# Seven products instead of eight in thirteen more places of a two-layer decoder trunk

## The chip, the cores and the metric

The kernel runs on one core of a Trainium2 chip. The metric is device time in microseconds of that core for one launch. Engines are named as the profile names them: PE is TensorE (matmul), PEld its weight loads, DVE is VectorE, ACT is ScalarE, POOL is GpSimd, SP is SyncE, whose queue issues the DMAs. PSUM is the accumulator memory that PE writes, in eight banks of 128 x 512 fp32.

## The reference

Two layers of a decoder on x of 256 rows by D = 2048, all in fp32. The first mixes with a gated short convolution, the second with stick-breaking attention of 16 heads; each is followed by a squared-ReLU MLP with a hidden width of 4 D. Keys and values are made once, after the first layer.

```
def short_conv_mixer(u, w_in, conv_w, w_out):            # layer 0
    xin, gate_c, gate_b = jnp.split(u @ w_in, 3, axis=-1)
    ...
    return (gate_b * conv) @ w_out
def sq_relu_mlp(u, w_up, w_down):
    return jnp.square(jax.nn.relu(u @ w_up)) @ w_down
def reference(...):
    for i in range(2):
        u = rmsnorm(h, mix_pre_g[i])
        m = short_conv_mixer(u, ...) if i == 0 else stick_breaking_mixer(u, w_q, k_sh, v_sh, w_o)
        h = h + rmsnorm(m, mix_post_g[i])
        u = rmsnorm(h, mlp_pre_g[i])
        h = h + rmsnorm(sq_relu_mlp(u, w_up[i], w_down[i]), mlp_post_g[i])
        if i == 0:
            k_sh, v_sh = split(rmsnorm(h, kv_norm_g) @ w_kv)
```

## The kernel before, in words

**Products.** fp32 numbers are split into a high part that PE takes exactly and a low part. A *product* is three 128 x 512 matmuls into one PSUM bank: high by high, high by low, low by high. Of each 128 x 1024 weight tile that arrives by DMA (`raw`, names `r...`), ACT makes the high part (`h...`, a rounding copy) and DVE the low part (`l...`, the subtraction). `hu`, `lu` belong to the up weights, `hd`, `ld` to the down weights, `hin`, `hout`, `hv`, `hk`, `hq`, `hwo` to the others. High and low parts have six pages each (`SLOTS`), so DVE and ACT can be at most six pages ahead of PE.

**Groups.** A `Group` computes 256 rows by 1024 columns over 2048 rows of a weight: two row blocks b, two column halves c, sixteen weight tiles, so 64 products into four banks `acc`. The groups run one after the other: six `in` groups, two `out`, then for each layer's MLP four quarters of two up groups and two down groups (`u<layer><quarter><group>`, `d...`), between the layers the value groups `v0` and `v1`, eight narrower groups for k and q, and two `wo` groups. In the kernel before, `v0` comes ahead of the k and q groups and `v1` behind them.

**Seven products.** Two weight tiles by two row blocks make a 2 x 2 block product, for which `seven` uses seven products instead of eight, with sums of operands: of the data (forms `us`, `hs`, `ys`, made once per norm or hidden tile by `make_forms`) and of the weights (`t1` to `t4`, made by DVE for every pair of tiles). A "seven" in this text is such a pair; an "eight" is an ordinary tile with four products, so two eights stand for one seven. Four of the seven products go to four extra banks `q`, so a group with sevens fills all eight banks. After a group's last seven `combine` makes the sums of the q banks on ACT and DVE, and after its last product `finals` adds them to `acc` on the way out. The lists `UP_SEVEN`, `DN_SEVEN` and so on say which of the eight pairs of a group are sevens; `turns` spreads them among the eights, with `FORE` eights ahead and `REAR` behind.

**First and last groups.** The first group behind a norm (`enter`) starts with its first four tiles (`EDGE`) for row block 0 alone, since row block 1 is not ready yet. The last group ahead of a norm (`leave`) does its last four tiles bank by bank, so that the norm can begin on the first banks while PE works on the others. In the kernel before, neither kind has sevens, nor do `v0`, `v1` and `wo`.

**Order.** `Plan` is a list scheduler that runs when the kernel is built: every instruction is a task with an estimated duration and a due time, and the plan fixes the order on each engine. On the chip each engine goes through its list in that order.

Lines of the profile: L643 is the matmul of a product, L407 every ACT instruction, L415 every two-operand DVE instruction, L422 DVE's form with a scalar, L466 the transposes.

Of the kernel before, what the change touches and what calls it, by code (L numbers as in the profile page):

```python
# [88 lines left out]
class Plan:  # L89
# [13 lines left out]
    def task(self, eng, dur, fn, reads=(), writes=(), side=False, soon=None, kb=0.0, table=None, own=(), after=()):  # L103
# [3 lines left out]
        t.preds, t.succs, t.allocs, t.kb, t.table, t.side = set(after), [], [], kb, table, side  # L107
# [59 lines left out]
    def place(self):  # L167
# [52 lines left out]
        while done < len(tasks):  # L220
# [39 lines left out]
            if e in ("SP", "POOL") and t.kb:  # L260
# [3 lines left out]
                t.end = dma + 1.9  # L264
# [59 lines left out]

UP_SEVEN = ((0,1,2,4),(0,1,2))
IN_SEVEN = (0,1,2)
OUT_SEVEN = (0,1,2)
DN_SEVEN = ((0,1,2,4),)*2
SUMS_BY_DMA = ()
# [4 lines left out]
UP_DMA = ((),)*2  # L334
IN_DMA = ()
OUT_DMA = ()
LO_DMA = "lo"
DN_DMA = ((),)*2
# [3 lines left out]
def trunk(ctx, tc, x, xT, vecs, rows, ws, hs, qs, out):  # L342
# [165 lines left out]

    def raw_page(name):
        return page("raw", [P, CW], F32, name)  # L510

    def split(raw, name, a=0, b=CW, parts=1, gains=None):
        hi, lo = page("hi", [P, CW], F32R, "h" + name), page("lo", [P, CW], F32R, "l" + name)
# [92 lines left out]
    def make_forms(XS, pairs, r0, r1, name, spare):  # L606
# [14 lines left out]
        for j in pairs:  # L621
# [11 lines left out]
            if place is None:  # L633
                XS["late"].append(last)
            else:
                last()
# [12 lines left out]
    class Group:  # L649


        def __init__(self, name, w, base, n, X, banks, evict, ks=1, gains=None, XS=None, sevens=(), seeds=None, qbanks=None, start=None, bydma=(), qin=None, qout=None):
            self.qin, self.qout = qin, qout
            self.bydma = bydma
            self.name, self.w, self.base, self.n, self.X, self.banks, self.evict = name, w, base, n, X, banks, evict
            self.ks, self.gains, self.XS, self.sevens, self.seeds, self.qbanks = ks, gains, XS, sevens, seeds, qbanks
            self.start, self.fine, self.on, self.before_out = start, 0, None, None
# [41 lines left out]
        def seven(self, j, last):  # L699
# [3 lines left out]
            if j in SUMS_BY_DMA:  # L703
                rs = page("rs", [P, CW], F32, f"r{name}s")
                r1 = page("r2", [P, HALF], F32, f"r{name}b")
                twice = w[base + 1][:, HALF:].unsqueeze(1).to_broadcast([P, 2, HALF])
                load(rs.col().as3("p (a n) -> p a n", a=2), twice)
                load_add(rs.col(), w[base])
                load(r0.col(), w[base])
                load(r1.col(), w[base + 1][:, :HALF])  # L710
                b22, b21, t1, t2, t4 = r0.col(HALF, CW), r1.col(), rs.col(0, HALF), r2.col(0, HALF), r2.col(HALF, CW)
                at = {"t1": (rs, 0), "t3": (rs, 1), "t2": (r2, 0), "t4": (r2, 1), "b21": (r1, 0)}
            else:
                r1 = raw_page(f"r{name}b")
                r3 = page("r2", [P, HALF], F32, f"r{name}d")
                load(r0.col(), w[base])
                load(r1.col(), w[base + 1])
                b11, b22, b21, b12 = r0.col(0, HALF), r0.col(HALF, CW), r1.col(0, HALF), r1.col(HALF, CW)
                t1, t2, t4 = r2.col(0, HALF), r2.col(HALF, CW), r3.col()
# [880 lines left out]
```

## Time and profile before

| | |
|---|---|
| time, median of three runs | 2111.51 us (2111.33 to 2111.85) |
| time of the profiled execution | 2110.88 us |
| span in its trace | 2109.2 us |
| granted clock of PE | 0.999 |
| PE busy | 2093.5 us, 99% |
| PEld busy | 1737.5 us, 82% |
| DVE busy | 1867.1 us, 89% |
| ACT busy | 1346.0 us, 64% |
| DMA | 429.67 MB, mean 204 GB/s |

Busy time is the union of an engine's instructions. The span runs from the first to the last instruction of the trace; the time of the execution has 1.7 us around it. Matmuls overlap each other in the records, so a mean duration (some 390 ns) is not the distance from one to the next, which the chain of waits gives.

### The profile page before, as it was taken

Reading aid. Unit: us, or ns where it says so; the run is one execution under the profiler, and the core shown is the slowest. Engines: PE = TensorE matmul, PEld = TensorE weight load, DVE = VectorE, ACT = ScalarE, POOL = GpSimd, SP = SyncE. Lnnn points to the kernel's source line nnn. Section 1 sums busy time; section 2 is a strip of 40 time slices with the busy share of each in tenths; the row PEclk is TensorE's granted clock in tenths of the full one; section 3 lists DMA queues with packets and bytes.
Section 4 is the critical chain, followed back from the end, with each engine's and each line's share of the span. In section 5 each row is a group of like instructions: output and inputs, shape, how many; then the busy total and the mean of one; then the engine's idle time right before and its main releaser. Section 6 shows DMA issues by size and latency. Waiting matters only on the chain.

```text
span 2109.2 us, 27197 instructions
## 1 busy us (share of the span) xinstructions
PE 2093.5 (99%) x9506; PEld 1737.5 (82%) x9506; DVE 1867.1 (89%) x2646; ACT 1346.0 (64%) x1933; POOL 1.0 (0%) x7
## 2 busy tenths in 40 slices
PE   8999999999999999999999999999999999999998
PEld 7888888888888888888888888888888888888886
DVE  6999996899999999999657777558999999999995
ACT  7665566765666575577657776447655765665673
POOL 0000000000000000000000000000000000000000
PEclk9999999999999999999999999999999999999999
DMA  8556676556656656657664555755566566656673
GB/s 330 196 194 201 209 257 221 178 185 216 200 184 212 204 190 204 216 189 279 226 193 158 163 164 174 236 189 200 185 198 228 181 198 203 218 180 201 200 269 120
DMA packets 119801, 429.67 MB, mean 204 GB/s; under 512 B 13296, under 2 KB 13424, under 8 KB 119664
## 3 DMA queue, kind: packets, MB, share of 16 engines
q1 hardware_dynamic: 119520, 427.87, 60.9%
q8 instruction: 74, 1.21, 0.2%
q14 instruction: 63, 0.52, 0.1%
q10 hardware_dynamic: 144, 0.07, 0.0%
HBM read 419.50 MB, written 8.39 MB: 203 GB/s over the span
## 4 chain that ended last, share of the span: by engine, by line
PE 98%; DVE 1%; ACT 0%; issue 0%; DMA 0%; DVEq 0%; ACTq 0%
PE acc L643 79%; PE q L643 16%; PE tr L466 2%; PE o L1424 0%; PE z L1374 0%; DVE lv L422 0%; DVE hh L422 0%; PE ex L1404 0%; ACT hid L407 0%; PE o L1425 0%; PE z L1375 0%; DMA gv<-vecs 0%; DVE u L415 0%; PE ex L1405 0%; ACT hu L407 0%
## 5 line engine op out<-in xcount | busy, mean ns | idle before, releaser
L643 PE MATMUL acc<-hu,u 128*128 128x512 f32 x1472 | 471.4, 392 | 0.0
L643 PE MATMUL acc<-hd,hid 128*128 128x512 f32 x1376 | 437.7, 391 | 0.0
L643 PEld LDWEIGHTS acc<-hu,u 128*128 128x128 f32 x1472 | 276.4, 188 | 56.4
L643 PEld LDWEIGHTS acc<-hd,hid 128*128 128x128 f32 x1376 | 258.5, 188 | 52.8
L643 PE MATMUL acc<-lu,u 128*128 128x512 f32 x736 | 286.7, 390 | 0.0
L643 PE MATMUL acc<-ld,hid 128*128 128x512 f32 x688 | 268.0, 389 | 0.0
L415 DVE TENSOR_TENSOR lu<-ru,hu 128x1024 fp32r<-128x1024 f32 x160 | 193.2, 1221 | 17.1 <-ACT hu L407 16.6
L407 ACT ACTIVATE hu<-ru 128x1024 fp32r<-128x1024 f32 x160 | 167.4, 1058 | 45.8 <-PE acc L643 31.2
L643 PE MATMUL acc<-hin,u 128*128 128x512 f32 x588 | 186.6, 393 | 5.8 <-ACT hin L407 5.8
L415 DVE TENSOR_TENSOR ld<-rd,hd 128x1024 fp32r<-128x1024 f32 x144 | 173.6, 1219 | 19.8 <-ACT hd L407 19.5
L407 ACT ACTIVATE hd<-rd 128x1024 fp32r<-128x1024 f32 x144 | 149.1, 1052 | 40.5 <-PE acc L643 34.4
L643 PEld LDWEIGHTS acc<-lu,u 128*128 128x128 f32 x736 | 138.4, 188 | 27.5
L643 PEld LDWEIGHTS acc<-ld,hid 128*128 128x128 f32 x688 | 129.3, 188 | 26.2
L643 PEld LDWEIGHTS acc<-hin,u 128*128 128x128 f32 x588 | 111.2, 189 | 28.8 <-ACT hin L407 6.1
L643 PE MATMUL acc<-lin,u 128*128 128x512 f32 x294 | 115.3, 392 | 0.0
L415 DVE TENSOR_TENSOR q<-acc,q 128x512 f32<-128x512 f32 x130 | 87.1, 689 | 7.4 <-PE acc L643 5.6
L415 DVE TENSOR_TENSOR q<-q,q 128x512 f32<-128x512 f32 x136 | 92.7, 682 | 0.5 <-ACT q L407 0.3
L643 PE MATMUL q<-hd,hs 128*128 128x512 f32 x240 | 92.1, 389 | 0.0
L643 PE MATMUL acc<-hk,u 128*128 128x512 f32 x256 | 86.6, 399 | 0.0
L415 DVE TENSOR_TENSOR lin<-rin,hin 128x1024 fp32r<-128x1024 f32 (+1 forms) x72 | 80.1, 1129 | 4.5 <-ACT hin L407 4.2
L643 PE MATMUL acc<-hv,u 128*128 128x512 f32 x256 | 82.9, 394 | 0.1
L407 ACT ACTIVATE hin<-rin 128x1024 fp32r<-128x1024 f32 (+1 forms) x72 | 69.8, 984 | 19.8 <-PE acc L643 9.9
(1656 smaller groups left out, 4476.1 us busy)
## 6 DMA issues: line engine op xcount, KB each, us to landing
ru<-w_up SPq DMA_DIRECT2D x160, 512.0 KB, 4.3
rd<-w_dn SPq DMA_DIRECT2D x144, 512.0 KB, 4.5
rin<-w_in SPq DMA_DIRECT2D x64, 512.0 KB, 4.7
rv<-w_v SPq DMA_DIRECT2D x32, 512.0 KB, 4.2
rk<-w_k SPq DMA_DIRECT2D x32, 512.0 KB, 4.2
rq<-w_q SPq DMA_DIRECT2D x32, 512.0 KB, 3.9
rwo<-w_wo SPq DMA_DIRECT2D x32, 512.0 KB, 4.3
rout<-w_out SPq DMA_DIRECT2D x26, 512.0 KB, 4.6
```

What stands on the lines that cost most here:

```text
L407: nc.scalar.activation(out_.w(), in_.r(), func, scale=val(scale), **more)
L415: "DVE", dve(width(out_)), lambda: nc.vector.tensor_tensor(out_.w(), a.r(), b.r(), op=op),
L466: nc.tensor.matmul(to.w(), src.r(), ident.tile[:], is_transpose=True, start=j == 0, stop=True, skip_group_check=True)
L643: nc.tensor.matmul(ps.w(), a.w(), w.w(), start=first and j == 0, stop=last and j == 2, skip_group_check=skip)
```

## The change

**Where sevens are added.** `UP_FIRST`: pair 7 of the first up group of each layer. `FIRST_SEVEN` is empty, so the first `in` group stays without. `OUT_LEAVE` and `DN_LEAVE`: pairs 0 and 1 of the last `out` group and of the last down group of each layer. `V_SEVEN`: pairs 3 to 7 of `v1`. That is 2 + 2 + 4 + 5 = 13. The up groups keep their number of sevens but on other pairs. (`UP_SEVEN[0]` goes from 0, 1, 2, 4 to 3, 5, 6, 7, `UP_SEVEN[1]` from 0, 1, 2 to 5, 6, 7.)

**Leaving groups with sevens.** In a group that leaves, `fold` has DVE add the combined sums to `acc` in PSUM, in place, ahead of the last four tiles; PE then accumulates on top.

**Weight sums.** One DVE instruction over 1024 columns, one of its inputs read twice, makes `t1` and `t3`; `t2` replaces the input. The product of q7 moves from fifth to second place and that of q6 from second to fifth, and the last two stay.

**Values and attention.** `v1` runs directly behind `v0`. Its norm `kv` gets forms for pairs 3 to 7 (high plus low part of the operand, then `make_forms`), and each seven of `v1` first has ACT scale the two raw tiles by the norm's gains in four pieces. All heads' outputs (`mixed`) are made within the k and q groups, where the last eight stood at the end of `v1`; the attention's buffers `lb` shrink from eight to six.

**What moves in the lists.** VectorE's list at the first seven of the second `in` group (`rin10a`, `rin10b` are the two raw tiles, `rin10c` the page of the wide sums, `rin10d` that of the last sum), before:

```order
L415 TENSOR_TENSOR rin10c<-rin10b,rin10a 128x512
L415 TENSOR_TENSOR rin10c<-rin10c,rin10a 128x512
L415 TENSOR_TENSOR rin10b<-rin10b,rin10a 128x512
L415 TENSOR_TENSOR rin10d<-rin10c,rin10b 128x512
L415 TENSOR_TENSOR lin_664<-rin10c,hin_652 128x1024
```

and now:

```order
L427 TENSOR_TENSOR rin10c<-rin10b,rin10a 128x1024
L427 TENSOR_TENSOR rin10b<-rin10c,rin10a 128x512
L427 TENSOR_TENSOR rin10d<-rin10b 128x512
L427 TENSOR_TENSOR lin_663<-rin10c,hin_646 128x1024
L427 TENSOR_TENSOR lin_681<-rin10a,hin_670 128x1024
```

Two narrow sums have become one wide one; every seven of the kernel has this change, old ones too.

VectorE's list behind the last tiles of `v0`, before, where the k group (`lk`) follows:

```order
L422 SCALAR_TENSOR_TENSOR lv_9764<-rv_9652,gv,hv_9754 128x1024
L422 SCALAR_TENSOR_TENSOR lv_9782<-rv_9660,gv,hv_9772 128x1024
L422 SCALAR_TENSOR_TENSOR lk_9798<-rk_9675,gv,hk_9790 128x512 x2
L422 SCALAR_TENSOR_TENSOR lk_9818<-rk_9702,gv,hk_9812 128x512 x2
L422 SCALAR_TENSOR_TENSOR lk_9838<-rk_9720,gv,hk_9832 128x512 x2
```

and now, in `v1`, the sevens of pairs 5 and 6, the second and third of four that follow each other without an eight between them (`rv15a` is the first raw tile of pair 5 in `v1`):

```order
L427 TENSOR_TENSOR lv_10073<-rv14d,hv_10067 128x512
L427 TENSOR_TENSOR rv15d<-rv15b 128x512
L427 TENSOR_TENSOR lv_10089<-rv15c,hv_10075 128x1024
L427 TENSOR_TENSOR lv_10099<-rv15a,hv_10087 128x1024
L427 TENSOR_TENSOR rv16c<-rv16b,rv16a 128x1024
L427 TENSOR_TENSOR lv_10118<-rv15b,hv_10094 128x1024
L427 TENSOR_TENSOR lv_10128<-rv15d,hv_10104 128x512
L427 TENSOR_TENSOR lv_10137<-rv16c,hv_10120 128x1024
```

Where VectorE had one instruction for each tile or two short ones, it has a block of sevens with seven instructions each.

VectorE's list at the end of the last down group of the first layer (`ld` are its last tiles, `lv` the first of `v0`), before:

```order
L415 TENSOR_TENSOR ld_9344<-rd_9245,hd_9336 128x1024
L415 TENSOR_TENSOR ld_9362<-rd_9255,hd_9354 128x1024
L415 TENSOR_TENSOR ld_9380<-rd_9267,hd_9372 128x1024
L422 SCALAR_TENSOR_TENSOR lv_9398<-rv_9280,gv,hv_9390 128x1024
L422 SCALAR_TENSOR_TENSOR lv_9416<-rv_9298,gv,hv_9406 128x1024
```

and now, with two of the combined sums and the four folds (`acc<-acc,q`):

```order
L427 TENSOR_TENSOR ld_9395<-rd_9276,hd_9376 128x1024
L427 TENSOR_TENSOR q_9369<-q_9369,q_9229 128x512
L427 TENSOR_TENSOR ld_9408<-rd_9318,hd_9383 128x1024
L427 TENSOR_TENSOR acc_9135<-acc_9135,q_9355 128x512
L427 TENSOR_TENSOR q_9422<-q_9369,q_9219 128x512
L427 TENSOR_TENSOR acc_9118<-acc_9118,q_9388 128x512
L427 TENSOR_TENSOR acc_9094<-acc_9094,q_9369 128x512
L427 TENSOR_TENSOR acc_9103<-acc_9103,q_9422 128x512
L434 SCALAR_TENSOR_TENSOR lv_9438<-rv_9328,gv,hv_9404 128x1024
```

The folds stand behind the low parts of the group's last tile and ahead of everything of the next group.

```diff
-SLOTS = {"raw": 7, "rs": 0, "rt": 1, ...
+SLOTS = {"raw": 7, "rt": 1, ...
...
 def seven(stage, i, q, j):
     if stage == "up":
-        return UP_SEVEN[j] if (q, j) != (0, 0) else ()
+        return UP_SEVEN[j] if (q, j) != (0, 0) else UP_FIRST
     if stage == "in":
-        return IN_SEVEN if j else ()
+        return IN_SEVEN if j else FIRST_SEVEN
     if stage == "out":
-        return OUT_SEVEN if j == 0 else ()
+        return OUT_SEVEN if j == 0 else OUT_LEAVE
     if stage == "dn":
-        return DN_SEVEN[j] if (q, j) != (QUARTERS - 1, 1) else ()
+        return DN_SEVEN[j] if (q, j) != (QUARTERS - 1, 1) else DN_LEAVE
+    if stage in ("v", "wo"):
+        return (V_SEVEN if stage == "v" else WO_SEVEN)[j]
     return ()
-UP_SEVEN = ((0,1,2,4),(0,1,2))
+UP_FIRST = (7,)
+V_SEVEN = ((),(3,4,5,6,7))
+WO_SEVEN = ((),())
+UP_SEVEN = ((3,5,6,7),(5,6,7))
 IN_SEVEN = (0,1,2)
+FIRST_SEVEN = ()
+OUT_LEAVE = (0,1)
+DN_LEAVE = (0,1)
 OUT_SEVEN = (0,1,2)
 DN_SEVEN = ((0,1,2,4),)*2
+AHEAD = 2
+LFORE = 3
+UP_FORE, V_FORE, WO_FORE, WO_REAR = 11,6,10,1
...
         def seven(self, j, last):
-                r1 = raw_page(f"r{name}b")
-                r3 = page("r2", [P, HALF], F32, f"r{name}d")
...
-                t1, t2, t4 = r2.col(0, HALF), r2.col(HALF, CW), r3.col()
-                at = {"t1": (r2, 0), "t2": (r2, 1), "t3": (r1, 1), "b21": (r1, 0), "t4": (r3, 0)}
-                tt(t1, b12, b11, ALU.add)
-                tt(b12, b12, b22, ALU.add)
+            if self.gains:
+                for v, k in ((b12, 0), (b11, 0), (b22, 1), (b21, 1)):
+                    act(v, v, AF.Copy, scale=self.gains(2 * j + k)[0])
+            t1, t4 = r2.col(0, HALF), r3.col()
+            tt(r2.col().as3("p (a n) -> p a n", a=2), b12.bc(2), r0.col().as3("p (a n) -> p a n", a=2), ALU.add)
+            t2 = b12
+            at = {"t1": (r2, 0), "t3": (r2, 1), "t2": (r1, 1), "b21": (r1, 0), "t4": (r3, 0)}
             tt(t2, t1, b22, ALU.add)
             tt(t4, t2, b21, ALU.add)
...
-        def mixed(self):
-            order = turns(self.sevens, PAIRS)
+        def mixed(self, enter=False, leave=False):
+            fore, rear = (LFORE, EDGE + AHEAD) if leave else (self.fore, self.rear)
+            order = turns(self.sevens, PAIRS, fore, rear)
+            upto = len(order) - (EDGE if leave else 0)
...
                 else:
                     for b in range(NB):
-                        self.unit(b, j, (kind, j) == order[-1])
+                        for c in range(2):
+                            self.half(b, c, j, (kind, j) == order[-1])
+                            if leave and z == upto - 1 and b == 0:
+                                self.fold(b, c)
+            if leave:
+                for b in range(NB):
+                    for c in range(2):
+                        if b or not AHEAD:
+                            self.fold(b, c)
+                        for kind, j in order[upto:]:
+                            self.half(b, c, j, (kind, j) == order[-1])
+                        self.finish(b, c)
...
+        def fold(self, b, c):
+            ps = self.ps[b, c].col()
+            s, op = self.ends()[b, c]
+            tt(ps, ps, s, op)
...
     class Norms:
                     for c in sorted({j // 2 for j in self.sevens}):
+                        for e in range(NB) if self.gain is None else ():
+                            r = self.raw[e, c] = page("c2", [P, 512], F32, "uraw")
+                            hi, lw = [piece(self.X, c, i, e) for i in range(2)]
+                            tt(r.col().as3("p (k t) -> p k t", k=4), hi, lw, ALU.add, soon=20.0)
                         make_forms(...)
...
-    kv = Norms("kv", B_MPOST0, hs, hs)
+    kv = Norms("kv", B_MPOST0, hs, hs, sets=[set(s) for s in (*V_SEVEN, ())])
...
-    groups = [values(0)]
+    groups = [values(0), values(1)]
     for j in range(4):
         ...
-    groups[1].start = to_attention
-    groups.append(values(1))
+    groups[2].start = to_attention
```

More of the change, by code (lines that the diff above doesn't have):

```diff
@@ L631, in last @@
                 both_parts(XS[j]["s1"], r1.col(at + P, at + 2 * P))
-            if place is None:
+            if place is None and j not in XS["first"]:
                 XS["late"].append(last)
@@ L778, in mixed @@
                     self.acc(b, c)
-            for kind, j in order:
+            if enter:
+                for b in range(NB):
+                    for kind, j in order[:EDGE]:
+                        self.unit(b, j)
+            for z, (kind, j) in enumerate(order[:upto]):
+                if enter and z < EDGE:
+                    continue
+                if self.on:
+                    self.on(order, z)
                 if kind == 7:
@@ L821, in whole @@
                 if self.on:
-                    self.on(i)
+                    self.on([(8, k) for k in range(self.n)], i)
                 for b in range(NB):
@@ L839, in turns @@
             m = len(rest)
-            a, b = (z * m // gaps, (z + 1) * m // gaps) if z < gaps else (m, m)
+            a, b = (z * m // gaps, (z + 1) * m // gaps) if z < gaps else (m if gaps else 0, m)
             order += rest[a:b]
-        return order + one[len(one) - REAR :]
+        return order + one[len(one) - rear :]
     def run(groups, enter=False, leave=False):
+        if len(groups) == 1 and groups[0].sevens:
+            groups[0].whole(enter, leave)
+            return
         units = [(gr, i) for gr in groups for i in range(gr.n)] if (enter or leave) else []
@@ L944, in enter @@
                 self.X[c] = operand(f"u{c}")
-            if any(j // 2 == c for j in self.sevens):
+            if any(j // 2 == c for j in self.sevens) and self.gain is not None:
                 self.raw[b, c] = page("c2", [P, 512], F32, "uraw")
@@ L1050, in enter, with arriving @@
                 make_forms_of(uS, k // 2, xpair[k // 2], "us", u4)
-        def arriving(k):
-            if k == 0:
-                for q in range(3):
-                    load_x(q)
-                enter(0)
-            if k % 2 == 0:
-                load_x(k // 2 + 3)
-            if k + 1 < KD:
-                enter(k + 1)
+        def arriving(order, z):
+            tiles = [k for kind, j in order[: z + 1 + EARLY] for k in ((j,) if kind == 8 else (2 * j, 2 * j + 1))]
+            pairs = list(dict.fromkeys(k // 2 for kind, j in order for k in ((j,) if kind == 8 else (2 * j,))))
+            now = order[z][1] // 2 if order[z][0] == 8 else order[z][1]
+            for q in pairs[: pairs.index(now) + 4 if z else 3]:
+                if q not in xpair:
+                    load_x(q)
+            if z == 0:
+                enter(order[0][1])
+                for q in pairs[:4]:
+                    if q not in xpair:
+                        load_x(q)
+            for k in tiles:
+                if k not in entered:
+                    enter(k)
         def statistics():
@@ L1074, in statistics @@
                 tt(t, r1[b], r1[b], ALU.mult)
-            hold()
-        def hold():
-            for n in range(SLOTS["dh"]):
-                p, s = page("dh", [P, CW], F32, "hold").col(0, 1), r1[n % NB]
-                plan.task("POOL", 0.3, lambda p=p, s=s: nc.gpsimd.tensor_copy(p.w(), s.r()), [s], [p])
         def turned(banks, c, srcs):
@@ L1474, in slots @@
                 weights(hd)
+            for hd in pair(b):
+                mixed(hd)
             tabled(plan.task("ACT", 0.05, lambda: None, table=TABLES[AF.Sqrt]))
-            A["rest"] = [hd for p in range(NH // 4, NH // 2) for hd in pair(p)]
     def k_gains(i, tiles):
@@ L1570 @@
     arrays["w_out"] = banded(a["a_w_out"][0], sevens=[seven("out", 0, 0, j) for j in range(2)])
-    arrays["w_wo"] = banded(a["b_w_o"][0])
+    arrays["w_wo"] = banded(a["b_w_o"][0], sevens=[seven("wo", 0, 0, j) for j in range(2)])
     for j in range(2):
-        arrays[f"w_v{j}"] = banded(a["w_kv"][:, D + j * CW : D + (j + 1) * CW])
+        arrays[f"w_v{j}"] = banded(a["w_kv"][:, D + j * CW : D + (j + 1) * CW], sevens=[seven("v", 0, 0, j)])
     for j in range(4):
```

177 lines of the change are left out of this document (96 added, 81 removed).

## The prediction

> **What bounds the kernel now.** The page first, for the share of each engine and of the chain of work that ended last.
>
> ```profile
> PE 2093.5 (99%) x9506; PEld 1737.5 (82%) x9506; DVE 1867.1 (89%) x2646; ACT 1346.0 (64%) x1933; POOL 1.0 (0%) x7
> PE 98%; DVE 1%; ACT 0%; issue 0%; DMA 0%; DVEq 0%; ACTq 0%
> ```
>
> PE fills the chain. Two views show that it also runs at a fixed pace. The chain in order of time (start, length, what) gives the distance from one matmul to the next, and the list of waits on PE (total, times, longest) what holds it up.
>
> ```profile
> 61.14 6.80 PE acc L643 x30
> ...
> 475.79 14.96 PE acc L643 x66
> ...
> 2057.99 42.85 PE acc L643 x189
> 2100.85 0.02 issue
> ```
>
> ```profile
> PE acc L643 <- ACT hin L407: 5.8, 1, 5.8
> PE q L643 <- ACT hid L407: 1.4, 2, 0.7
> ```
>
> 6.80 / 30 = 14.96 / 66 = 42.85 / 189 = 0.2267 us for a matmul, early, in the middle and at the end. PE waits for its first operand (5.8) and twice 0.7 us later on; behind its last matmul at 2100.8 lie 8.3 us of norm. Every matmul taken from PE's list is thus worth 0.2267 us, a product 0.680, as long as DVE and ACT deliver. So the next thing to read is how much room they have, in the stages that the change touches (columns: stretch, its length, then busy time of PE, PEld, DVE and ACT).
>
> ```profile
> 351.40:398.60 47.20, 47.20 (x226) 39.09 (x224) 43.71 (x86) 37.14 (x85) 0.00 (x0) 1.00 0.65 219
> 398.60:443.80 45.20, 44.51 (x210) 36.82 (x208) 39.34 (x59) 29.82 (x44) 0.00 (x0) 1.00 0.57 185
> 443.80:485.00 41.20, 41.20 (x187) 34.15 (x185) 41.01 (x57) 28.95 (x39) 0.00 (x0) 1.00 0.58 193
> 485.00:526.00 41.00, 41.00 (x183) 33.97 (x182) 40.52 (x49) 22.70 (x26) 0.00 (x0) 1.00 0.62 205
> ...
> 987.50:1032.00 44.50, 44.50 (x202) 36.95 (x201) 29.06 (x38) 21.35 (x29) 0.00 (x0) 1.00 0.60 212
> 1032.00:1078.80 46.80, 46.67 (x217) 38.38 (x216) 32.57 (x45) 31.05 (x53) 0.00 (x0) 1.00 0.72 234
> 1078.80:1278.10 199.30, 199.30 (x936) 166.05 (x935) 137.60 (x270) 138.19 (x231) 0.00 (x0) 1.00 0.52 169
> ```
>
> These are the first two up groups of layer 0, its first two down groups, the last down group (`d031`), `v0`, and the k and q groups. In the MLP's later groups DVE is idle for 0.2 to 0.5 us of 41, yet PE never waits: DVE needs just as long as PE and stays ahead by its pages. How little ahead, the timeline of the last quarter shows:
>
> ```profile
> 2037.94 0.68 DVE L415 TENSOR_TENSOR rd1304c<-rd1304b,rd1304a 128x512 f32<-128x512 f32 x1
> 2038.55 0.68 DVE L415 TENSOR_TENSOR ld<-rd1302d,hd 128x512 fp32r<-128x512 f32 x1
> ...
> 2039.75 1.22 DVE L415 TENSOR_TENSOR ld<-rd,hd 128x1024 fp32r<-128x1024 f32 x1
> ...
> 2041.74 0.39 PE L643 MATMUL acc<-ld,hid 128*128 128x512 f32 x1
> ```
>
> The low part that is ready at 2039.75 + 1.22 = 2040.97 is used at 2041.74, 0.77 us later. The first two rows show that neighbours on DVE overlap by 0.07 us (0.61 from start to start). The prices of DVE's and ACT's instructions (count, busy time, mean ns):
>
> ```profile
> L415 DVE TENSOR_TENSOR lu<-ru,hu 128x1024 fp32r<-128x1024 f32 x160 | 193.2, 1221 | 17.1 <-ACT hu L407 16.6
> L415 DVE TENSOR_TENSOR q<-q,q 128x512 f32<-128x512 f32 x136 | 92.7, 682 | 0.5 <-ACT q L407 0.3
> L415 DVE TENSOR_TENSOR q<-acc,q 128x512 f32<-128x512 f32 x130 | 87.1, 689 | 7.4 <-PE acc L643 5.6
> L422 DVE SCALAR_TENSOR_TENSOR lv<-rv,gv,hv 128x1024 fp32r<-128x1024 f32 x32 | 40.8, 1280 | 19.4 <-ACT hv L407 19.4
> L415 DVE TENSOR_TENSOR lm<-lm,causal 128x256 f32<-128x256 f32 x16 | 6.7, 417 | 0.1
> L415 DVE TENSOR_TENSOR hs<-hid,hs 128x256 fp32r<-128x256 f32 x32 | 12.9, 419 | 0.0
> L415 DVE TENSOR_TENSOR uraw<-uraw 128x128 f32<-128x128 f32 x16 | 4.4, 287 | 0.3
> L407 ACT ACTIVATE hu<-ru 128x1024 fp32r<-128x1024 f32 x160 | 167.4, 1058 | 45.8 <-PE acc L643 31.2 <-issue 7.9 <-PE q L643 4.3
> L407 ACT ACTIVATE hk<-rk,gv 128x512 fp32r<-128x512 f32 x64 | 43.2, 717 | 35.4 <-PE acc L643 31.2 <-issue 4.2
> L407 ACT ACTIVATE hv<-rv,gv 128x1024 fp32r<-128x1024 f32 x32 | 36.5, 1148 | 24.0 <-PE acc L643 24.0
> ```
>
> **The change, part by part.** *Removed products.* Thirteen sevens, three matmuls each: the list of 128x512 matmuls goes from 8866 to 8827 while transposes and attention matmuls keep their numbers. 39 x 0.2267 = 8.84 us. A smaller value would need a stage in which PE is not the pace, treated below. The page "TensorE: Matmul & The Clock Gate" of the Trainium skill gives, in its section on the back-to-back issue gap, about 131 ns for a matmul of 512 columns in a sustained stream; by it the 39 would bring an estimated 5.1 us and the time would come out near 2106.4. The trace has 226.7 ns in every dense stretch, so the sum goes by that.
>
> *A seven on DVE and ACT.* DVE: one wide sum (1.22, priced as any 1024 columns; reading one input twice costs nothing in the nearest row, `lm<-lm,causal`, whose mask is read twice, 417 against 419 ns for plain 256 columns), two narrow sums (2 x 0.68), three wide low parts (3 x 1.22) and a narrow one (0.68): 6.92 us. The two eights that it replaces take 2 x 1.22 = 2.44, so an added seven costs DVE 4.48 us for 0.68 us of PE. A seven of before had four narrow sums, 7.06, so each old one gets 0.14 us cheaper.
>
> *First up groups.* One seven (4.48), `combine` (4 x 0.682 = 2.73) and the four exits that become DVE adds (4 x 0.689 = 2.76): 9.97 us more on DVE, per layer. Idle there from 351.4 to 485: 3.49 + 5.86 + 0.19 = 9.54, plus 7 x 0.14 = 1.0 for the cheaper sums of the next two groups: 10.5. It fits by half a microsecond, before the overlap of the 13 extra instructions (0.9). From then on each group has 0.14 x 4 = 0.56 us more room than before. I take no stall; bounds 0 and what rival two gives. The two 0.7 us waits are PE's first product into a `q` bank behind these groups, whose bank ACT has not yet emptied. Now these groups end as all others with sevens do, which show no such wait. Bounds 0 and -1.4; I take -1.0.
>
> *Last groups.* In `d031` DVE gets 2 x 4.48 + 2.73 + 4 x 0.689 for the folds = 14.4 us onto 29.06, in 44.5 - 1.4 = 43.1 us: 43.5, less 18 overlaps of 0.07, 42.2. It fits. A fold of row block 0 can start when its bank's last product ahead of the final four tiles is done; PE has three products, 2.04 us, before it needs the bank, and the fold takes about 0.69 (nearest row `q<-acc,q`, which also reads PSUM). The folds stand behind the last low part, which is a page bound by the seven before and ready well ahead of that, since two eights (5.4 us) lie between. Bounds 0 and all twelve folds exposed, 12 x 0.69 = 8.3; I take 0.2. The norm behind the last matmul (8.3 us) is unchanged.
>
> *`v0` and `v1`.* In `v0` DVE makes the forms: six sums of 512 (4.1), eight of 256 and four of 128 columns (3.35 + 1.15), five low parts of 256 and ten of 128 (2.1 + 2.9), 13.6 us. `v0` has 46.8 - 32.57 = 14.2 free, and some of its 32.57 belongs to the k tiles, which now come later. In `v1` the sevens cost 5 x 6.92 and the eights 6 x 1.28, with `combine` 45.0 us, less 45 overlaps 41.9, against 59 x 0.680 = 40.1 on PE. ACT has four extra scalings for each seven (4 x 0.717), so 4 x 0.717 + 3 x 1.058 + 0.6 (a narrow copy, taken between half of 1.058 and 0.717) = 6.6, and 5 x 6.6 + 6 x 1.148 = 40.1: it too needs all of PE's time. What covers the shortfall is the start that DVE has from `v0`, at most the six pages, one seven and a half (1.5 x 4.76 = 7.1 us). Bounds: 0, and 6.4 us if that start is missing, since four sevens stand in a row and each takes DVE 6.92 - 7 x 0.07 = 6.4 against 7 x 0.680 = 4.76. Nearer to the start's 7.1, I take 0.8. What is late next if it stalls: the k group, whose stage has 62 us of idle DVE, so nothing is passed on. The weight loads keep their number (802 wide ones on SP), `v1`'s now run directly behind those of `v0`; their stage moved 234 GB/s at 72% before, so I cost them at nothing, covered by seven raw pages. The heads' outputs that move into the k and q groups are the same number of matmuls as before, and DVE (137.6 of 199.3) and ACT (138.2) have room for the rest of that work.
>
> **The sum.** 2110.88 (profiled; span 2109.2 and 1.7 around it) - 8.84 - 1.0 + 0.8 + 0.2 = 2102.0. The median of the runs shown, 2111.51, is 0.63 above the profiled execution; with it 2102.7, or -0.42%. A change of this kernel under about 0.2% (4.2 us) can't be told from none.
>
> **Rivals.** *One: DVE or ACT paces `v1`.* For it: both are at 40 us of 40 there, with four sevens in a row. Against: the start from `v0` and a slack stage behind. Without the start, 2102.7 - 0.8 + 6.4 = 2108.3; half of it, 2105.
>
> *Two, slower: DVE becomes the bound of the MLPs.* The 9.97 us in each first up group find only idle time that cannot be used (DVE waiting for pages or for PE), and all later groups have DVE at 99%, so the debt is never repaid and shows as PE's wait wherever the head start is thinnest. Less that 0.77, it gives (9.97 - 0.77) x 2 = 18.4: 2121. It decides against the change from 4.4 us a layer on. For it: 41.01 of 41.20. Against: 0.56 us more room a group, and 7.4 us of idle time in the two up groups stands right where the new work is. The page "Perfetto Trace Analysis" of the Trainium skill, in "Identifying the Most-Contended Engine", would take TensorE's weight-load share instead of its matmul share; by that (82% against DVE's 89%) DVE is the engine to relieve and this rival the rule. The constant 0.2267 us speaks against it.
>
> *Three: the folds are exposed.* 2102.7 - 0.2 + 8.3 = 2110.8, no change. Against: 2.04 us for 0.69.
>
> *Four: better still.* Both waits go and `v1` does not stall: 2102.7 - 0.4 - 0.8 - 0.2 = 2101.3, and some 0.8 less where PE starts `v0` in step with DVE. That the change removes nothing is excluded by the list's 39 matmuls.
>
> **Chances.** Forecast as summed, 2101.0 to 2104.5: 0.66. Rival one, 2104.5 to 2108.3: 0.14, of which 0.10 is still faster by over 0.2% (below 2107.3). Rival two: 0.06, slower. Rival three: 0.04, same. Rival four: 0.10. So faster 0.86, same 0.08, slower 0.06. The range leaves out the far parts of rivals one, two and three and reaches down to rival four: 2100.4 to 2107.4.
>
> **What the profile would show.** Right: PE with 39 fewer matmuls at 0.2267 us, about 2084.7 us busy; no wait of `q` on `hid`; at most a microsecond of PE waiting for `lv` or `hv`; DVE over 95% busy in the first two up groups; folds done before their product. Wrong: PE waiting for `lu` or `ld` in the first quarter, for `acc` behind a fold, or `v1` taking over 42 us.

## The result, and the profile after

The changed kernel takes 2100.01 us (median of six runs, 2099.43 to 2100.4) against 2111.57 (six runs, 2111.33 to 2112.0) for the kernel before: ratio 0.9945, 95% interval 0.9932 to 0.9958. It is faster by 0.55%, where 0.42% was forecast, and 0.4 us below the low end of the range. The profiled execution took 2100.11 us, its span is 2098.4 us.

The page of the changed kernel, busy times and the chain of work that ended last (in its line numbers L664 is the matmul of a product, L419 ACT's instruction, L427 and L434 DVE's):

```profile
PE 2084.3 (99%) x9467; PEld 1730.1 (82%) x9467; DVE 1936.9 (92%) x2668; ACT 1378.9 (66%) x2002; POOL 1.0 (0%) x7
PE 99%; DMA 0%; DVE 0%; ACT 0%; issue 0%; DVEq 0%; ACTq 0%
```

PE has 39 matmuls fewer and is the whole chain. All its waits of any size are in one line:

```profile
PE acc L664 <- ACT hin L419: 5.9, 1, 5.9
```

That is the wait for the first operand. The two waits of `q` for `hid` are gone, and no wait for `lv`, `ld`, `lu` or for a fold has come. The stages that the change touches, by stretch (length, then PE, PEld, DVE and ACT): the first two up groups, the first down group, the last down group of layer 0, `v0`, `v1`.

```profile
350.61:397.12 46.51, 46.51 (x223) 38.48 (x221) 45.67 (x86) 38.50 (x87) 0.00 (x0) 1.00 0.63 215
397.12:440.41 43.29, 43.29 (x203) 35.97 (x201) 42.22 (x62) 29.66 (x45) 0.00 (x0) 1.00 0.59 194
440.41:482.66 42.25, 42.25 (x195) 35.09 (x194) 42.13 (x55) 28.66 (x40) 0.00 (x0) 1.00 0.60 199
...
985.08:1028.14 43.06, 43.06 (x196) 35.75 (x194) 40.35 (x55) 26.20 (x36) 0.00 (x0) 1.00 0.62 209
1028.14:1074.50 46.36, 46.36 (x218) 38.45 (x217) 45.80 (x77) 38.71 (x72) 0.00 (x0) 1.00 0.67 226
1074.50:1114.62 40.12, 40.12 (x179) 33.23 (x178) 36.05 (x43) 34.65 (x48) 0.00 (x0) 1.00 0.51 171
```

`v1` takes 40.12 us, which is its 59 products at 0.680. The last down group lost 1.36 of its 44.4 us, which is its two products, so its folds cost nothing. DVE is 98% busy in the first up groups and nobody waits for it.

Where the 10.8 us of span went, group by group (each from its first matmul to that of the next group, before against after, less the matmuls removed at 0.2267):

| place | beyond the removed matmuls, us |
|---|---|
| 39 matmuls | -8.84 |
| second up group and first down group, layer 0 and layer 1 | -1.03 and -1.06 |
| `v0` | -0.43 |
| attention: `v1` moved, heads' outputs moved | +0.18 |
| first `in` group | +0.58 |
| all the rest, with the norm at the end | -0.2 |

Against the forecast, two gains are larger, around the `q` wait (2.1 instead of 1.0) and at the start of `v0` (0.43, not in the sum), and the two costs that the sum held (`v1` 0.8, folds 0.2) did not come. The first `in` group, which gets no seven, is spread between executions (last section).

### The profile page after: what moved, and what is told of

Read it like the earlier page. It is cut to its first block, busy times and chain, and to the rows that moved or that the text cites. A ratio compares the mean times of both kernels' runs of the same rounds, so it can differ in the third digit from the quotient of the medians.

```text
span 2098.4 us, 27237 instructions
## 1 busy us (share of the span) xinstructions
PE 2084.3 (99%) x9467; PEld 1730.1 (82%) x9467; DVE 1936.9 (92%) x2668; ACT 1378.9 (66%) x2002; POOL 1.0 (0%) x7
## 4 chain that ended last, share of the span: by engine, by line
PE 99%; DMA 0%; DVE 0%; ACT 0%; issue 0%; DVEq 0%; ACTq 0%
PE acc L664 78%; PE q L664 17%; PE tr L478 2%; PE z L1424 0%; PE o L1477 0%; PE ex L1454 0%; PE o L1478 0%; PE z L1425 0%; DMA gv<-vecs 0%; DVE hh L434 0%; PE ex L1455 0%; PE ey L1459 0%; ACT u L419 0%; DVE mg L434 0%; DVEq L1657 0%
## 5 line engine op out<-in xcount | busy, mean ns | idle before, releaser
L664 PE MATMUL acc<-hu,u 128*128 128x512 f32 x1448 | 463.2, 391 | 0.0
L664 PE MATMUL acc<-hd,hid 128*128 128x512 f32 x1328 | 424.5, 391 | 0.0
L664 PEld LDWEIGHTS acc<-hu,u 128*128 128x128 f32 x1448 | 271.9, 188 | 55.7 <-DVE u L434 0.4
L664 PEld LDWEIGHTS acc<-hd,hid 128*128 128x128 f32 x1328 | 249.3, 188 | 51.0
L664 PE MATMUL acc<-lu,u 128*128 128x512 f32 x724 | 281.8, 389 | 0.0
L664 PE MATMUL acc<-ld,hid 128*128 128x512 f32 x664 | 258.4, 389 | 0.0
L427 DVE TENSOR_TENSOR lu<-ru,hu 128x1024 fp32r<-128x1024 f32 x156 | 188.4, 1218 | 7.4 <-ACT hu L419 7.2
L664 PE MATMUL acc<-hin,u 128*128 128x512 f32 x588 | 187.0, 393 | 5.9 <-ACT hin L419 5.9
L419 ACT ACTIVATE hu<-ru 128x1024 fp32r<-128x1024 f32 x156 | 162.0, 1055 | 30.9 <-PE acc L664 15.8
L427 DVE TENSOR_TENSOR ld<-rd,hd 128x1024 fp32r<-128x1024 f32 x136 | 164.0, 1217 | 4.0 <-ACT hd L419 3.9
L664 PEld LDWEIGHTS acc<-lu,u 128*128 128x128 f32 x724 | 136.0, 188 | 27.3
L664 PEld LDWEIGHTS acc<-ld,hid 128*128 128x128 f32 x664 | 124.8, 188 | 25.0
L419 ACT ACTIVATE hd<-rd 128x1024 fp32r<-128x1024 f32 x136 | 139.1, 1049 | 5.4 <-PE acc L664 4.2
L664 PEld LDWEIGHTS acc<-hin,u 128*128 128x128 f32 x588 | 111.5, 190 | 28.9 <-ACT hin L419 5.9
L664 PE MATMUL acc<-lin,u 128*128 128x512 f32 x294 | 115.4, 393 | 0.0
L427 DVE TENSOR_TENSOR q<-q,q 128x512 f32<-128x512 f32 x160 | 108.9, 680 | 2.1 <-PE q L664 0.9
L427 DVE TENSOR_TENSOR q<-acc,q 128x512 f32<-128x512 f32 x142 | 92.4, 685 | 4.6 <-PE acc L664 3.8
L664 PE MATMUL q<-hd,hs 128*128 128x512 f32 x248 | 95.8, 389 | 0.0
L664 PE MATMUL q<-hd,hid 128*128 128x512 f32 x232 | 90.2, 389 | 0.0
L664 PE MATMUL acc<-hk,u 128*128 128x512 f32 x256 | 87.1, 399 | 0.0
L427 DVE TENSOR_TENSOR lin<-rin,hin 128x1024 fp32r<-128x1024 f32 (+1 forms) x72 | 80.3, 1130 | 5.8 <-ACT hin L419 5.4
L419 ACT ACTIVATE hin<-rin 128x1024 fp32r<-128x1024 f32 (+1 forms) x72 | 69.7, 983 | 23.9 <-PE acc L664 11.1
```

The lines of the kernel that those rows point to most:

```text
L419: nc.scalar.activation(out_.w(), in_.r(), func, scale=val(scale), **more)
L427: "DVE", dve(width(out_)), lambda: nc.vector.tensor_tensor(out_.w(), a.r(), b.r(), op=op),
L664: nc.tensor.matmul(ps.w(), a.w(), w.w(), start=first and j == 0, stop=last and j == 2, skip_group_check=skip)
```

## The experiments

All times are medians. The kernel before had 2111.55, 2111.52 and 2111.63 us in the three series, so differences between series can be read to some tenths.

| kernel | us | ratio to before, 95% interval |
|---|---|---|
| changed kernel | 2100.01 | 0.9945 (0.9932 to 0.9958) |
| e4_none: no added pair | 2109.52 | 0.9990 (0.9981 to 0.9999) |
| e6_before_fore4: before, first seven later | 2109.45 | 0.9990 (0.9981 to 0.9999) |
| e3_no_first: without the pair in the first up groups | 2102.19 | 0.9955 (0.9943 to 0.9968) |
| e5_old_sums: narrow sums, old product order | 2100.89 | 0.9949 (0.9936 to 0.9961) |
| g1_before_q7: before, new product order | 2113.46 | 1.0009 (1.0000 to 1.0018) |
| g2_none_q6: e4_none, old product order | 2112.75 | 1.0006 (0.9997 to 1.0015) |
| h1_old_first: narrow sums, old order, one pair | 2108.17 | 0.9985 (0.9976 to 0.9994) |
| e1_no_v: no pairs in `v1` | 2104.25 | 0.9965 (0.9951 to 0.9978) |
| e10_no_ahead: folds not ahead | 2103.88 | 0.9963 (0.9951 to 0.9976) |
| e9_leave3: three pairs in the last down groups | 2104.05 | 0.9964 (0.9951 to 0.9976) |
| e7_v_seven7: seven pairs in `v1` | 2109.97 | 0.9994 (0.9985 to 1.0003) |
| e8_first4: four pairs in the first up groups | 2116.89 | 1.0024 (1.0015 to 1.0034) |

### What took the wait for `q` away

The wait's place in the kernel before: ACT's and PE's rows at the second up group (start, length, engine and line, out<-in).

```profile
405.37 1.06 ACT L407 ACTIVATE hu<-ru 128x1024 fp32r<-128x1024 f32 x1
406.40 0.60 ACT L407 ACTIVATE hid<-tr 128x512 f32<-128x512 f32 x1
...
405.77 0.60 PE L466 MATMUL tr<-ident,relu 128*128 128x128 f32 x4
407.06 0.50 PE L643 MATMUL q<-hu,us 128*128 128x512 f32 x1 [0.69 <-ACT hid L407]
407.39 0.40 PE L643 MATMUL q<-lu,us 128*128 128x512 f32 x1
```

The bank of q6, the second product of a seven, still holds the transposes of the last hidden tile, which ACT empties at 406.40 to 407.00, behind a weight tile. From the transposes to the product PE takes 1.29 us (405.77 to 407.06); without a wait the same step takes 0.35 (below). The wait listed as 0.69 thus costs 0.94.

**e4_none** and **e3_no_first**. Lists of pairs emptied in the changed kernel, all four in e4_none (shown), `UP_FIRST` alone in e3_no_first:

```diff
-UP_FIRST = (7,)
-V_SEVEN = ((),(3,4,5,6,7))
+UP_FIRST = ()
+V_SEVEN = ((),())
...
-OUT_LEAVE = (0,1)
-DN_LEAVE = (0,1)
+OUT_LEAVE = ()
+DN_LEAVE = ()
```

> The change without its thirteen added sevens: the lists UP_FIRST, V_SEVEN, OUT_LEAVE and DN_LEAVE are empty, all else (cheaper weight sums, the order of products, v1 behind v0, the up groups' pairs) stays. My theory: the removed products are worth 13 x 0.680 = 8.84 us and the q-bank wait of the first up groups (0.94 us a layer) goes only because these groups now leave by DVE additions; only the wait in v0 (0.43) goes without sevens. So this kernel is 0.0 to 0.6 us below before, near 2111.2, and the trace shows PE's first q product behind the first up group waiting again. Rival: the reordering itself (other pairs, wide sums) took away the waits; then 2109.2, 2.3 below before.

> The change without the seven in the first up group of each layer (UP_FIRST empty), all else kept. My theory: two products come back (1.36 us) and with them the q-bank wait behind the first up group (1.9 us): 2100.0 + 3.2 = 2103.2. Rival: the wait went for another reason (pairs, cheaper sums); then only the products come back, 2101.4.

The theory of e4_none fell: without any added pair the time is 2109.52, 2 us below before, and PE's list of waits has no `q` in it. Rows of e4_none at the same place:

```profile
406.24 1.06 ACT L419 ACTIVATE hu<-ru 128x1024 fp32r<-128x1024 f32 x1
407.27 0.60 ACT L419 ACTIVATE hid<-tr 128x512 f32<-128x512 f32 x1
...
406.64 0.60 PE L478 MATMUL tr<-ident,relu 128*128 128x128 f32 x4
406.99 0.48 PE L664 MATMUL q<-hu,us 128*128 128x512 f32 x1
...
408.92 0.39 PE L664 MATMUL acc<-hu,us 128*128 128x512 f32 x1
409.15 0.39 PE L664 MATMUL q<-hu,us 128*128 128x512 f32 x1
```

ACT is no earlier: it empties the bank 1.23 us behind the transposes, as before (407.87 against 406.64). But the product at 406.99 is now that of q7, in another bank. q6 is fifth, at 409.15. e3_no_first keeps the other eleven pairs and also shows no wait. Its median, 2.2 above the changed kernel, lies between theory and rival; its trace is 1.6 us longer, of which 1.36 are the two products, and the second up and first down group gain 0.93 in each layer (1.03 and 1.06 in the changed kernel). Both kernels keep what else the change sets, the plan's estimates among it, so that these two runs don't yet show that the order of products alone suffices; g1 below does.

**e6_before_fore4.** The kernel before, with the second up group's first seven behind four ordinary tiles:

```diff
-            order = turns(self.sevens, PAIRS)
+            order = turns(self.sevens, PAIRS, getattr(self, 'fore', FORE))
...
+                if (q, j) == (0, 1):
+                    gr.fore = 4
```

> The kernel before, with one edit: the second up group of each layer has four eights ahead of its first seven instead of two, so that PE has other work until ACT has emptied the q bank. No product is removed. My theory: the wait costs 0.94 us a layer (0.83 ahead of the first q matmul and 0.11 behind it), so 1.9 us in all: 2109.7. Rival: the wait only moves to the next thing that is late (a low part, or the bank of another q product), and the time stays at 2111.5.

2109.45: the two waits are worth 2 us, not the 1.4 that the list gives.

**e5_old_sums.** All thirteen pairs, with the four narrow sums and q6 second again:

```diff
-            tt(r2.col().as3("p (a n) -> p a n", a=2), b12.bc(2), r0.col().as3("p (a n) -> p a n", a=2), ALU.add)
-            t2 = b12
...
+            tt(t1, b12, b11, ALU.add)
+            tt(b12, b12, b22, ALU.add)
...
             prod(q(5), "q5", s("s1"), "t1")
-            prod(q(7), "q7", s("s3"), "t3")
+            prod(q(6), "q6", s("s2"), "t2")
...
-            prod(q(6), "q6", s("s2"), "t2")
+            prod(q(7), "q7", s("s3"), "t3")
```

> The change with the four narrow weight sums of before and the old order of products, all thirteen added sevens kept. Each seven takes VectorE 0.07 us more from start to start (0.14 busy), 135 sevens in all. My theory: VectorE stays ahead of TensorE nearly everywhere, and the sums paid for little: 2100.0 to 2102.0, with any wait in v1, where the low parts are only 0.64 us ahead, or in the last down groups. Rival: the added sevens are affordable only because the sums became cheaper; then PE waits for low parts through the MLPs and the time is 2105 or more.

0.9 above the changed kernel, in the theory's range, and again no wait for `hid`, although q6 is second. So the order is not the only thing that removes it. Two runs turn the order alone, one on each side.

**g1_before_q7** and **g2_none_q6.** The edit of g1 in the kernel before; g2 has the reverse one in e4_none:

```diff
             prod(q(5), "q5", s("s1"), "t1")
...
-            prod(q(6), "q6", s("s2"), "t2")
+            prod(q(7), "q7", s("s3"), "t3")
...
-            prod(q(7), "q7", s("s3"), "t3")
+            prod(q(6), "q6", s("s2"), "t2")
```

> The kernel before with one edit: in every pair the products of q6 and q7 change places, so q7 is second and q6 fifth. The four narrow sums, the lists of pairs, the exits and the estimates stay. Theory (the place of q6 in the list is the cause): the bank of q6 is emptied by ACT at about 407.0, a seven's fifth product starts 4 x 0.68 = 2.7 us after its first, so PE no longer waits for it; both waits of 0.69 go and what belonged to them, as in the kernel with four ordinary tiles ahead: 2109.5, ratio 0.999. Rival (the exits, the wide sums or the estimates take the wait away): PE q <- ACT hid stays in the list at 1.4 us and the time at 2111.5. Third: the wait moves from q6 to the bank of q7, with less than 0.7 us: about 2110.5.

> The changed kernel without all thirteen added pairs (2109.5 when it was timed), and with the old places of q6 (second) and q7 (fifth). Wide sums, pairs and estimates of the changed kernel stay. Theory: the wait of PE's q product for ACT's hid is back with about 0.7 us in each layer, 2111.2 to 2111.5. Rival: no wait, 2109.5.

On the wait both came out as the theory says: g1 has none, g2 has it back. PE's waits, first of g1, then of g2:

```profile
PE acc L643 <- ACT hin L407: 5.8, 1, 5.8
PE q L643 <- DVE ld L415: 1.0, 6, 0.2
```

```profile
PE acc L664 <- ACT hin L419: 6.0, 1, 6.0
PE q L664 <- ACT hid L419: 1.4, 2, 0.7
PE q L664 <- DVE ld L427: 0.3, 2, 0.2
```

In g1 the second up and first down group together lose 0.93 us in each layer. The times are higher all the same, 2113.46 and 2112.75, since both kernels now wait for low parts of down groups. (Against before, g1's interval starts at 1.0000 and g2's holds it; the groups' lengths carry the reading.) Of g1, a seven of a down group, DVE's rows and then PE's:

```profile
638.18 1.22 DVE L415 TENSOR_TENSOR ld<-rd0104b,hd 128x1024 fp32r<-128x1024 f32 x1
639.32 1.22 DVE L415 TENSOR_TENSOR ld<-rd0104a,hd 128x1024 fp32r<-128x1024 f32 x1
...
640.02 0.40 PE L643 MATMUL q<-hd,hid 128*128 128x512 f32 x1
640.59 0.50 PE L643 MATMUL q<-ld,hid 128*128 128x512 f32 x1 [0.17 <-DVE ld L415]
640.93 0.40 PE L643 MATMUL q<-hd,hid 128*128 128x512 f32 x1
```

The narrow sums put `t1` and `t2` on one page, the wide sum `t1` and `t3`. In each kernel as made, the first two products read one page. When only the order is changed, the second product already needs the second page (`b`) and the third product the third (`a`); in each kernel as made, the second page is needed at the third product and the third at the fifth, so they are due one and two products (0.68 and 1.36 us) earlier. The low part of `a` ends at 639.32 + 1.22 = 640.54, its use is at 640.59. DVE's smallest head start in the down groups (from the end of a low part's row to the first matmul that reads it, over all low parts) is 0.05 us in g1 and g2, against 0.77 in the kernel before and 1.12 in the changed one (there in the last down groups, 1.55 in the others). Each such stall shows 0.2 in the list and costs about 0.6: in g1 each of the three later quarters of a layer is 0.57 to 0.72 us longer than before. Wide sum and new order belong together. In time the pair is worth little: e5, which has neither, has a trace 0.58 us longer than the changed kernel's, and 0.47 of that stand in the first `in` group, which neither edit touches. What the pair gives is head start in the down groups, where e5's smallest is 0.63.

**h1_old_first.** Narrow sums and old order as in e5_old_sums, without any of the added pairs but the one in the first up groups (the differences to the changed kernel are those of e5_old_sums and of e4_none, with `UP_FIRST = (7,)` kept).

> The changed kernel with the four narrow sums and the old product order (q6 second), and of the thirteen added pairs only the one in the first up group of each layer. By counts against the kernel before: 2 x 0.68 = 1.36 less. Theory (the exits of the first up groups, which become VectorE's adds, also suffice to take away PE's wait for ScalarE at the next group's q6): the wait is gone, 0.94 more for each layer, 2108.2. Rival (only the later place of q6 takes it away): the wait stays with 0.7 in each layer, 2110.1.

2108.17, on the theory. So the reason that the prediction gave is sufficient too. ACT's rows of h1 at that exit, and PE's second product:

```profile
402.04 1.08 ACT L419 ACTIVATE hid<-tr 128x512 f32<-128x512 f32 x2
...
407.02 0.39 PE L664 MATMUL q<-hu,us 128*128 128x512 f32 x1
```

With a seven in the group ahead, the last three of its exits are DVE adds at 399.0 to 400.9, the transposes follow at once (the last at 401.4), and ACT has emptied the last bank at 403.1, four microseconds ahead of q6. The wait is gone twice over in the changed kernel: either part alone removes it.

### What the sevens cost at their places

**e1_no_v.** `V_SEVEN = ((),())`, the rest as changed.

> The changed kernel without the five pairs in v1 (with v1 still behind v0). Theory: five products of 0.680 are 3.40 us, as v1 took 59 x 0.680 in the trace of the changed kernel, so 2103.4, ratio 0.996; and 0.4 more, 2103.8, if PE's wait of 0.4 at the start of v0 comes back with it. Rival (VectorE or ScalarE did cost time in v1 or behind it, spread so thin that no wait is listed): less, 2102.5.

4.24 above the changed kernel: 3.40 by products, and `v0` is 0.45 longer again; the other 0.4 lies within the spread of the runs. This is the row `v0` of the table above. DVE's and PE's rows in the kernel before, near the end of `v0`'s entry:

```profile
1045.93 1.26 DVE L422 SCALAR_TENSOR_TENSOR lv<-rv,gv,hv 128x1024 fp32r<-128x1024 f32 x1
1047.11 0.68 DVE L415 TENSOR_TENSOR u<-tr,u 128x512 fp32r<-128x512 f32 x1
...
1047.33 0.39 PE L643 MATMUL acc<-lv,u 128*128 128x512 f32 x1
1047.85 0.73 PE L643 MATMUL acc<-hv,u 128*128 128x512 f32 x2
```

and DVE's in the changed kernel:

```profile
1041.97 0.68 DVE L427 TENSOR_TENSOR u<-tr,u 128x512 fp32r<-128x512 f32 x1
...
1042.64 0.67 DVE L427 TENSOR_TENSOR u<-tr,u 128x512 fp32r<-128x512 f32 x1
1043.22 3.69 DVE L427 TENSOR_TENSOR uraw<-u 128x512 f32<-128x512 f32 x6
```

Before, a late piece of the norm's output (`u`) stands behind a low part of weights and ends at 1047.79, and PE uses it at 1047.85. With sevens in `v1` the forms (`uraw`) are wanted, the `u` pieces are placed ahead of the weights, and the same piece is done at 1043.31.

**e10_no_ahead.** All folds behind the last ordinary tile ahead of the final four:

```diff
-AHEAD = 2
+AHEAD = 0
...
-                            if leave and z == upto - 1 and b == 0:
+                            if leave and AHEAD and z == upto - 1 and b == 0:
```

> The changed kernel, where in the leaving groups all four folds come behind the last of the ordinary tiles ahead of the final four, none of them two tiles earlier, so that PE needs a bank as soon as VectorE has folded it. Theory (folds cost nothing because PE has other products in between): with the cover gone PE waits for the first fold, 0.69 and the way from PE to VectorE and back, 1 to 1.5 us in each of three groups, then 0.69 for a fold against 2.7 us of PE for a bank, so none behind it: 2103 to 2104.5. Rival (the sums in PSUM are covered by whatever stands in PE's queue): 2100.0, no change. Second rival (each fold is exposed): 12 x 0.69, 2108.

2103.88, within the theory's range. PE's row at the first fold of the last down group, and the waits of the run:

```profile
1017.97 0.47 PE L664 MATMUL acc<-hd,hid 128*128 128x512 f32 x1 [0.31 <-DVE acc L427]
```

```profile
...
PE acc L664 <- DVE acc L427: 0.9, 3, 0.3
PE acc L664 <- DVE lu L427: 0.4, 1, 0.4
...
```

One fold of four is exposed in each leaving group, by 0.47 (start to start 0.70 instead of 0.23). With what follows it in the group that is 0.56, 1.07 and 0.59 us. The first up group of layer 0 loses 1.38 more and `v0` 0.44, because DVE comes later to their operands. The theory had 1 to 1.5 us in each of the three groups and nothing behind them, so that the time fell into its range is in part luck. DVE's folds in the changed kernel:

```profile
1015.16 0.69 DVE L427 TENSOR_TENSOR acc<-acc,q 128x512 f32<-128x512 f32 x1
...
1016.35 1.88 DVE L427 TENSOR_TENSOR acc<-acc,q 128x512 f32<-128x512 f32 x3
```

The first is done at 1015.85 and all four at 1018.23. The final four tiles begin 16 products (10.9 us) before the group's end at 1028.14, at 1017.26, and need a further bank every 2.72 us. The folds are free because they are early, by the cover that the prediction named.

**e9_leave3** (`DN_LEAVE = (0,1,2)`), **e7_v_seven7** (`V_SEVEN = ((),(1,2,3,4,5,6,7))`) and **e8_first4** (`UP_FIRST = (3,5,6,7)`, `UP_FORE` from 11 to 5) go on where the change stops.

> The changed kernel with three pairs instead of two in the last down group of each layer. Two products fewer, 1.36 us. Theory (VectorE's idle time in these groups, 2.7 of 43.1 and 5.0 of 42.2 us, and its head start there, 3.4 us and more behind the first pair, can be used): 4.2 us more in each group fit, 2098.7, at most 0.7 of it lost in the first. Rival (idle time of VectorE there is bound by pages and can't be used): PE waits 2 to 4 us for ld or for the folds, 2102.

> The changed kernel with seven pairs in v1 instead of five. Two products fewer for PE, 1.36 us. Theory (v1 lives on the head start that VectorE brings from v0): the low parts are 9.5 us ahead at v1's start now and 0.64 near its end; two more pairs cost VectorE about 5.4 us of forms in v0, where it has 0.6 idle, and 2 x (6.4 - 4.76) = 3.3 in v1, so PE waits some 3.3 + 4.8 - 0.64 = 7.4 for low parts: 2106 (2103 to 2107), slower than the changed kernel. Rival (VectorE's list can give way, no stall in v1 at all): 2098.7.

> The changed kernel with four pairs instead of one in the first up group of each layer (3, 5, 6, 7, with five ordinary tiles ahead). Six products fewer, 4.08 us. Theory (VectorE's room there is used up): 3 x 4.48 less 1 of overlaps = 12.4 us more for VectorE in 2.0 us less, against 0.84 + 1.07 of idle time in the two up groups and about 3 of head start: some 9.5 us of waits for lu in each layer, 2100 + 2 x 7.5 = 2115, slower than before. Rival (VectorE does not set the pace, its 99% is only time that it fills): 2095.9.

All three lose. PE's waits of each, in this order, without the first operand's:

```profile
PE acc L664 <- DVE ld L427: 2.6, 4, 0.8
```

```profile
PE acc L664 <- DVE q L427: 2.5, 1, 2.5
PE acc L664 <- DVE lv L434: 1.8, 1, 1.8
PE acc L664 <- DVE lv L427: 1.3, 2, 0.8
PE q L664 <- DVE lv L427: 0.9, 3, 0.4
```

```profile
PE q L664 <- ACT us L419: 7.7, 4, 3.7
...
PE acc L664 <- DVE lu L427: 2.5, 6, 0.6
...
```

e9: the rival was right about the wait (2.6 us for `ld`), with a time 2 us above its 2102. DVE has 2.7 us idle in that group in the changed kernel and can't use them all for more sevens. The first of PE's waits there, and DVE's row for the last low part of the third seven, which shows DVE waiting for a high part from ACT:

```profile
1003.81 0.50 PE L664 MATMUL acc<-ld,hid 128*128 128x512 f32 x1 [0.54 <-DVE ld L427]
...
1009.15 0.69 DVE L427 TENSOR_TENSOR ld<-rd0312d,hd 128x512 fp32r<-128x512 f32 x1 [0.78 <-ACT hd L419]
```

The low part that PE wants at 1003.81 is an ordinary tile's, which DVE makes from 1002.54 to 1003.76, behind the third seven's wide sum. The 0.78 us are no wait for a page, as the rival had it: ACT makes the high part from the sum that DVE ends at 1008.38, and DVE needs it next in its list. Each last down group loses 2.47 us for the 0.68 that it saves. e7: 10 us above the changed kernel, where 6 were expected (3 to 7). The place is as expected (`v0` +3.8, `v1` +7.5 beyond the products); what I had missed is the sums of `v1`'s q banks, for which the k group's first bank waits (2.5), and the clock behind a stall (last section). e8: 2116.89, 2 us above the theory's 2115, through DVE's list as expected, though the wait listed first is for the forms `us`, which ACT makes from DVE's `uraw`. The first up group of layer 0, in stretch form as above:

```profile
350.80:406.05 55.25, 48.53 (x210) 37.02 (x209) 54.16 (x99) 40.46 (x90) 0.00 (x0) 0.97 0.49 171
```

DVE is busy for 54.16 of 55.25 us and PE for 48.53. That is the prediction's rival two, three pairs further on. The page "Perfetto Trace Analysis" of the Trainium skill, in "Identifying the Most-Contended Engine", judges TensorE by MFU and weight loads; by the weight loads it would have DVE relieved first. In the changed kernel (82% of weight loads against 92%) the trace doesn't bear it out; in this stretch (67% against 98%) it does.

No kernel of the study beats the changed one.

## Why the prediction was wrong

- *Removed products, -8.84.* Right: 39 matmuls, and each place lost its products at 0.680 to within 0.05 us.
- *Wait for `q`, -1.0.* This step failed, by size: it is worth 2.1 (1.9 where no pair is added, e4). The step took 1.0 out of 0 to 1.4 as a hedge between a wait that stays and one that goes, and took the listed 0.69 for the cost, where start to start it is 0.94. The cause it gave (the exits of the first up groups) is shown sufficient by h1. But it read the waiting product as PE's first into a `q` bank; it is the second, q6, and the step did not see that q6's new place removes the wait by itself (g1).
- *`v1`, +0.8.* Mis-sized: 0. The low parts are 9.5 to 11 us ahead at its start (estimated 7.1 from the pages of sevens alone, while `v1` opens with two eights, each page of which lasts PE 2.72 us) and 0.64 at the closest, near its end. It fits, and e7 shows that it fits by little.
- *Folds, +0.2.* 0, for the reason given.
- *`v0`.* The sum had no term; only rival four had some 0.8 where PE starts `v0` in step with DVE. It was 0.43, through the place of `u` ahead of the weights.
- *MLP stall, 0.* Right, but narrowly: DVE is at 97 to 98% in the first two up groups, as foreseen, and its smallest head start in the first of them is 0.40 us. In the down groups it is 1.12 or more (0.77 before).
- *PE's busy time*, foreseen at 2084.7, is 2084.3.
- *Resolution.* No run shows the 0.2% under which the prediction could not tell a change from none: the intervals here reach 0.09 to 0.13% to each side.

Remade with the measured terms the sum is 2111.51 - 8.84 - 2.09 - 0.43 = 2100.15 against 2100.01. Every one of the three open terms had been set against the change, each by a little (1.1, 0.8 and 0.2), and `v0` was left out (0.43). Together that is 2.5, more than the 2.3 from the forecast to the range's low end. Rival four, with 0.10, was the case that came, with the full price of the waits on top.

## What to carry to other kernels

A wait that a list of waits gives as 0.7 is priced start to start from the rows around it: in a dense stream it cost a third more here, and stalls listed at 0.2 cost 0.6. Where a product order and the layout of its operands are changed together, cost them together: each alone brought waits for low parts (g1, g2) that the two together don't have. And when one edit removes the cause of a wait in two ways, leave the hedge out: it takes both to fail before the wait stays.

## What the runs showed of the hardware

*PE at half pace behind a stall.* In e7 PE waits 1.8 us in `v0`, and 1.5 us later eight matmuls in a row stand 0.43 us apart instead of 0.2267; the granted clock (third column from the right) in that stretch is 0.66.

```profile
1062.44 0.50 PE L664 MATMUL acc<-lv,u 128*128 128x512 f32 x1 [1.83 <-DVE lv L434]
...
1064.37 1.05 PE L664 MATMUL acc<-hv,u 128*128 128x512 f32 x2
1065.22 0.63 PE L664 MATMUL acc<-lv,u 128*128 128x512 f32 x1
```

```profile
1062.40:1067.40 5.00, 4.96 (x15) 3.91 (x16) 5.00 (x5) 1.52 (x2) 0.00 (x0) 0.66 0.69 231
```

Eight matmuls at 0.2 us more are 1.6 us, almost the price of the stall over again. The stall of 2.5 us at the first k group has no such wake, so not every one is followed by it. The page "TensorE: Matmul & The Clock Gate" of the Trainium skill, in "The HAM clock gate", has two clocks, with 426.7 and 215.7 ns for a matmul of 512 columns, and a window that runs freely, so that the point of the change varies. The 0.43 agrees; the fast pace here is 226.7 ns. In e8 the wait of 3.7 us for `us` has such a wake too: from 379.60 to 383.00 us the granted clock is 0.50.

*The first group varies by itself.* 4 to 11 matmuls at the start of the first `in` group stand 0.43 apart, and its length goes from 45.16 (e10) to 46.61 us (h1) although every kernel has the same products there. The stretch from 6 to 12 us of the kernel before and of h1, with 19 and 14 matmuls in it:

```profile
6.00:12.00 6.00, 6.00 (x19) 4.49 (x20) 5.31 (x15) 5.30 (x14) 0.00 (x0) 1.00 0.99 366
```

```profile
6.00:12.00 6.00, 5.94 (x14) 4.48 (x15) 5.25 (x14) 5.30 (x15) 0.00 (x0) 1.00 0.98 364
```

The clock column reads 1.00 in both, since it counts the time ahead of the trace's first clock record as full. That record, a grant of the full clock, stands at 9.40 us in the kernel before, at 12.22 in h1 and at 8.93 in e10, and in all fourteen traces the spacing of 0.43 ends within 0.3 us of it. So this is the clock as well, granted 3.0 to 6.2 us behind the first matmul. The spread of a kernel's runs, 1 to 1.7 us, is of that size, and the 0.63 us between the profiled execution of before and its median lies within it; that the clock makes this spread too isn't shown, since one execution of each kernel has a trace.
